# Attention's output kept as features by queries, with the RMS factors as rows through DRAM

## The chip, the cores and the metric

The kernel runs on one core of one Trainium2 chip. The core has five engines with a queue each: PE (TensorE, matmuls; its weight loads are listed as PEld and overlap), DVE (VectorE), ACT (ScalarE), POOL (GpSimd) and SP (SyncE, which here only issues DMAs). Each takes its instructions in program order; they meet by semaphores. The metric is the device time of one execution in microseconds (us), the median of several.

## The reference

One layer of a diffusion backbone for 256 prompt tokens and 2048 sample tokens with 512 cached keys; 1024 features, 4 attention heads of width 128. The part that matters here is differential attention, its sub-norm and the output projection:

```python
s = einsum('bqhmd,bkhmd->bhmqk', q, k) * scale     # two score maps, m = 0, 1
p = softmax(s, axis=-1)
a = p[:, :, 0] - lam * p[:, :, 1]
o = einsum('bhqk,bkhe->bqhe', a, v)                # 128 features a head
a = rms_norm(o, subln_g) * (1.0 - lam_init)        # over the 128 features
x = x + g1 * (concatenate([a.reshape(b, n, 512), four], axis=-1) @ w_out)
```

The other 512 columns of the concatenation (`four`) come from a Fourier mixing done earlier. An MLP follows. Everything is float32 at the borders; most products are done as three matmuls of a high and a low part (`mm3`).

## The kernel before

The stages follow each other: modulation, norm and input projection, Fourier mixing, attention (about 553 to 1245 us of the profiled execution), W_out (to about 1470), MLP.

**Attention.** A head has 8 groups of 256 sample queries (`Group`), and one group of the 256 prompt queries (`Prompt`). A group has two halves j of 128 queries. For each j and each map m there are five blocks b of 512 keys: `fill` (PE writes scores to one of five PSUM banks, tag "S"), `rowmax` and `comb` (DVE), `exp` (ACT, which frees the bank). When both maps of a half are done, `combine` adds them: two sums on DVE, then six POOL operations, of which four are large. Then `tr` transposes the result, `ah` (ACT) and `al` (DVE) split it, and `mul` sums features x queries into columns 0:256 of the PSUM bank that `PRO()` returns, the one all groups share; the prompt has columns 256:512 of it. The end of a group is o1 to o6: o1, ACT copies to `oT`; o2, PE transposes it back, two of 128x128; o3, DVE copies to `o` (queries x features); o4, ACT squares with accumulation, two; o5, DVE and a pow on POOL (L91, `pow_mhalf`); o6, POOL scales the rows by their factors, two, and SP stores them to `att`, one DRAM tensor for each 128 tokens.

**What sets the order.** The attention stage is written as a list of (time, function). `add(t, fn)` appends, the list is sorted by time, and the functions run in that order; so each engine's program order is fixed, and an engine that waits holds all that stands behind it. One step T is 5.2, a group takes four; u = T/5. In such units after the start of its last part (w, L1335) a group has o1 at 0, o2 at 0.4, o3 at 4.25, o4 at 8.5, o5 at 9.2, o6 at 9.6; w of the next group is 20 later. The prompt's own end falls at group 5 of its head (G[5]). Tiles come from pools: a tag has `bufs` buffers, taken in turn, and a new tile of the tag waits until the readers of the one that had its buffer are done. The default of pool `at` is two. The last group of the last head (`gr.last`) leaves o2 to o6 to the list `LASTO`, which the W_out stage calls; there POOL also issues the DMAs.

**W_out.** For each of 18 tiles of 128 tokens, `mix_load` (L1558) loads `am` from `att` and four 128-feature blocks of `mT` from `four`; `mix` (L1565) transposes `am` on PE (four of 128x128), ACT copies with the sub-norm's gain (`cols[:, 96:97]`, features on partitions) into `mT`, DVE splits `mT`; `out_mm` multiplies with the split weights that `w_split` (L1540) makes once. The first tile's transposes stand at the end of attention (`mix0_load`, `mix0_tr`, `mix0_copy`).

Of the kernel before, what the change touches and what calls it, by code (L numbers as in the profile page):

```python
# [11 lines left out]
F32 = mybir.dt.float32  # L12
# [25 lines left out]
def f32(ap):  # L38
    return ap.bitcast(F32)


def body(tc, a, out):
    nc = tc.nc
    ctx = ExitStack()
    with ctx:
# [6 lines left out]
        def scratch(name, shape):  # L52
            return dram.tile(shape, F32, tag=name, name=name)
# [8 lines left out]
        att = [scratch(f"att{i}", [P, 512]) for i in range(NT // P)]  # L62
# [926 lines left out]
        with ExitStack() as c3_:  # L989
# [49 lines left out]
            class Group:  # L1039
# [133 lines left out]

                def o2(self):
                    for j in range(2):
                        nc.tensor.transpose(self.po[:, 256 + j * P:256 + j * P + P], self.oT[:, j * P:j * P + P], ident)

                def o3(self):
                    self.o = self.op.tile([P, 256], F32, tag="o", name=f"o{self.nm}")
                    nc.vector.tensor_copy(self.o, self.po[:, 256:512])  # L1180

                def o4(self):
                    osq = self.op.tile([P, P], F32, tag="osq", name=f"osq{self.nm}", bufs=1)
                    self.oss = self.op.tile([P, 4], F32, tag="oss", name=f"oss{self.nm}")
                    for j in range(2):
                        nc.scalar.activation(osq, self.o[:, j * P:j * P + P], AF.Square, accum_out=self.oss[:, j:j + 1])

                def o5(self):
                    nc.vector.scalar_tensor_tensor(self.oss[:, 0:2], self.oss[:, 0:2], 1.0 / P, self.s0e, op0=ALU.mult, op1=ALU.add)
                    pow_mhalf(self.oss[:, 2:4], self.oss[:, 0:2], 2)  # L1190

                def o6(self):
                    for j in range(2):
                        c = slice(j * P, j * P + P)
                        nc.gpsimd.tensor_scalar(self.o[:, c], self.o[:, c], self.oss[:, 2 + j:3 + j], 0.0, op0=ALU.mult, op1=ALU.add)
                        (nc.gpsimd if self.last else nc.sync).dma_start(att[self.hd.tok0 + self.g * 2 + j][:, self.hd.hc], self.o[:, c])

            class Prompt(Group):
# [39 lines left out]
                def mul(self, j):  # L1238

                    (ah, al), V = self.A[0], self.hd.V  # L1240
                    n = 0
                    for t in range(2):
                        c = slice((t * 2 + j) * P, (t * 2 + j) * P + P)
                        for l, r in ((ah[:, c], V[:, t, 0, :]), (ah[:, c], V[:, t, 1, :]), (al[:, c], V[:, t, 0, :])):
                            n += 1
                            nc.tensor.matmul(PRO()[:, 256 + j * P:256 + j * P + P], l, r, start=False, stop=(n == 6), skip_group_check=True)

                def o3(self):
                    self.o = self.op.tile([P, 256], F32, tag="o", name=f"o{self.nm}")
                    nc.vector.tensor_copy(self.o, PRO()[:, 256:512])  # L1250

# [9 lines left out]
            def load_wout():  # L1261
                ak = aks[0]
                wv = a["w_out"][0].rearrange("(k p) n -> p k n", p=P)
                ts = [ak.tile([P, NK[0]], F32R, tag=f"KS{m}_0", name=f"wout{m}") for m in range(2)]
                ts.append(ak.tile([P, NK[0] // P, 2, P], F32R, tag="V_0", name="wout2").rearrange("p t x e -> p (t x e)"))
                for n, k in ((0, 0), (0, 1), (1, 2), (1, 3), (2, 4), (2, 5), (2, 6), (2, 7)):
                    w = f32(ts[n])[:, k % 2 * D:k % 2 * D + D] if n < 2 else f32(ts[n])[:, (k - 4) * D:(k - 3) * D]
                    nc.sync.dma_start(w, wv[:, k, :])
                    WOUT.append(w)

                MIX0.extend((f32(ts[0])[:, 2 * D:2 * D + 512], f32(ts[2])[:, 4 * D:5 * D].rearrange("p (k t) -> p k t", t=P)))
                nc.sync.dma_start(MIX0[1][:, 4:8, :], four[:, 0:P].rearrange("(k p) t -> p k t", p=P))

            def mix0_load():
                nc.sync.dma_start(MIX0[0], att[0])

            def mix0_tr(gr):
                MIX0.append(gr.bank("pmx0", "pt"))
                for k in range(4):
                    nc.tensor.transpose(MIX0[2][:, k * P:k * P + P], MIX0[0][:, k * P:k * P + P], ident)  # L1280

            def mix0_copy():
                nc.scalar.activation(MIX0[1][:, 0:4, :].rearrange("p k t -> p (k t)"), MIX0[2], AF.Copy, scale=cols[:, 96:97])

            for h in range(H):
# [237 lines left out]
        with c3o, ExitStack() as c4, ExitStack() as c4x, ExitStack() as c4w:  # L1523
# [16 lines left out]
            def w_split(hf, k0=0, k1=KD):  # L1540
                c = slice(hf * 512, hf * 512 + 512)
                wh, wl = WO[hf]
                for k in range(k0, k1):
                    nc.scalar.copy(wh[k], WOUT[k][:, c])
                    nc.vector.tensor_sub(wl[k], WOUT[k][:, c], f32(wh[k]))
# [12 lines left out]
            def mix_load(i):  # L1558
                am = tx.tile([P, 512], F32, tag="am", name=f"am{i}")
                nc.sync.dma_start(am, att[i])  # L1560
                mT = tx.tile([P, 8, P], F32, tag="mT", name=f"mT{i}")
                nc.sync.dma_start(mT[:, 4:8, :], four[:, i * P:i * P + P].rearrange("(k p) t -> p k t", p=P))
                M[i] = am, mT

            def mix(i):  # L1565
                if i == s0:
                    mT = MIX0[1]
                else:
                    am, mT = M[i]
                    pm = PRO().rearrange("p (k t) -> p k t", t=P)  # L1570
                    for k in range(4):
                        nc.tensor.transpose(pm[:, k, :], am[:, k * P:k * P + P], ident)
                    nc.scalar.activation(mT[:, 0:4, :], pm, AF.Copy, scale=cols[:, 96:97])
# [558 lines left out]
```

## Time and profile before

| what | us |
|---|---|
| median of 3 runs | 2862.14 (2862.11 to 2862.57) |
| span of the profiled execution | 2861.4 |
| PE busy | 2831.7 (99%) |
| DVE, ACT, POOL busy | 2018.0, 1548.2, 1073.3 |
| attention, 553 to 1245 | 692, of which PE is busy 689.0, POOL 627.5 |
| W_out, 1250 to 1480 | 230, of which PE is busy 227.2 |

In the profile's lines, L1172 is line 1172 of the kernel before; in a line of operations stand the start, the duration, the engine, the line, output <- inputs by their names (numbers left out: `oTs` is the sample's `oT` of any head and group, `oTp` the prompt's), the shape, and in brackets an idle time before it with what ended it. A line of waits has who waits, for whom, the us in total, how often, and the longest. PE's rows overlap, since matmuls are pipelined: what a matmul costs is the step from one start to the next.

### The profile page before, as it was taken

How to read it: one execution, taken by the hardware profiler on the slowest of the kernel's cores; microseconds unless marked ns; L12 is line 12 of the kernel's file. 1: busy time of each engine (PE TensorE's matmuls, PEld its weight loads, DVE VectorE, ACT ScalarE, POOL GpSimd, SP SyncE). 2: the span in 40 equal slices, each digit the busy share in tenths (PEclk: the TensorE clock that was granted, in tenths of full speed). 3: DMA queues.
4: the chain of work that ended last, by engine and by line, in shares of the span. 5: the costliest groups of instructions: out<-in, count | busy, mean ns of one | idle time of the engine just before them, and what ended most of it. 6: DMA issues, size and time to landing. Idle time of an engine off the chain costs nothing.

```text
span 2861.4 us, 43224 instructions
## 1 busy us (share of the span) xinstructions
PE 2831.7 (99%) x15109; PEld 2455.9 (86%) x15109; DVE 2018.0 (71%) x3393; ACT 1548.2 (54%) x3505; POOL 1073.3 (38%) x890
## 2 busy tenths in 40 slices
PE   8999999999999999999999999999999999999999
PEld 5888888688888888888889999999998888888887
DVE  7767886898988989864477777778775354345554
ACT  4333323798989989853356565556555332333221
POOL 1211223798999989942223333333332000000000
PEclk9999999999999999999999999999999999999999
DMA  7776777421211212036767676667747464445663
GB/s 284 219 207 198 230 213 237 172 106 38 73 71 53 106 38 99 23 124 201 242 221 232 223 246 228 221 219 238 234 167 255 147 202 135 138 144 185 206 206 111
DMA packets 392780, 492.94 MB, mean 172 GB/s; under 512 B 26467, under 2 KB 306384, under 8 KB 389490
## 3 DMA queue, kind: packets, MB, share of 16 engines
q1 hardware_dynamic: 387136, 479.73, 50.9%
q0 software_dynamic: 1872, 7.28, 0.8%
q10 hardware_dynamic: 3554, 3.17, 0.4%
q8 instruction: 119, 1.95, 0.3%
q14 instruction: 99, 0.81, 0.1%
HBM read 312.58 MB, written 179.59 MB: 172 GB/s over the span
## 4 chain that ended last, share of the span: by engine, by line
PE 54%; DVE 1%; DMA 0%; ACT 0%; issue 0%; SPq 0%; POOL 0%; DVEq 0%; POOLq 0%
PE ps L94 8%; PE ps L95 8%; PE ps L96 8%; PE pB L1749 2%; PE pB L1747 2%; PE pB L1748 2%; PE pA L1748 2%; PE pC L1748 2%; PE pA L1749 2%; PE pC L1747 2%; PE pA L1747 2%; PE pC L1749 2%; PE po L94 2%; PE po L96 2%; PE po L95 2%; PE pD L1749 1%
## 5 line engine op out<-in xcount | busy, mean ns | idle before, releaser
L1085 DVE TENSOR_REDUCE mxs<-Ss 128x1 f32<-128x512 f32 x636 | 405.4, 686 | 65.5 <-PE Ss L1080 55.1
L1420 DVE TENSOR_TENSOR sl<-sr,sh 128x768 fp32r<-128x768 f32 x168 | 161.8, 964 | 331.5 <-ACT sh L1419 331.1
L1120 POOL TENSOR_TENSOR P0s<-P0s,P1s 128x1024 f32<-128x1024 f32 (+2 forms) x128 | 378.6, 2958 | 10.7
L1419 ACT CAST sh<-sr 128x768 fp32r<-128x768 f32 x168 | 140.6, 838 | 418.3 <-PE ps L95 418.3
L1789 POOL TENSOR_TENSOR gs<-g,g 128x384 f32<-128x384 f32 x48 | 69.7, 1452 | 468.5 <-ACT g L1759 418.9
L1104 ACT ACTIVATE P1s<-Ss,mxs 128x512 f32<-128x512 f32 x318 | 215.4, 694 | 36.3 <-DVE mxs L1088 35.3
L94 PE MATMUL pj<-wh,hh 128*128 128x512 f32 x576 | 228.8, 397 | 2.0 <-DVE hh L555 2.0
L94 PE MATMUL ps<-thT,sh 128*128 128x512 f32 x585 | 227.6, 389 | 0.0
L95 PE MATMUL ps<-tlT,sh 128*128 128x512 f32 x585 | 227.6, 389 | 0.0
L96 PE MATMUL ps<-thT,sl 128*128 128x512 f32 x585 | 227.6, 389 | 0.0
L95 PE MATMUL pj<-wl,hh 128*128 128x512 f32 x576 | 227.1, 394 | 0.5 <-DVE wl L516 0.5
L96 PE MATMUL pj<-wh,hl 128*128 128x512 f32 x576 | 225.6, 392 | 0.0
L1104 ACT ACTIVATE P0s<-Ss,mxs 128x512 f32<-128x512 f32 x318 | 214.3, 691 | 5.6 <-DVE mxs L1088 5.0
L1135 PE MATMUL pts<-ident,P0s 128*128 128x128 f32 x1280 | 191.7, 273 | 4.5 <-DVE als L1147 1.8
L1080 PE MATMUL Ss<-KS0s,Qs 128*128 128x512 f32 x636 | 190.1, 419 | 0.4 <-ACT P1s L1104 0.4
L1080 PE MATMUL Ss<-KS1s,Qs 128*128 128x512 f32 x636 | 188.7, 420 | 1.5 <-ACT P0s L1104 1.4
L1758 ACT ACTIVATE g<-uz 128x384 f32<-128x384 f32 x144 | 75.7, 526 | 200.2 <-DVE uz L1781 174.1
L1135 PEld LDWEIGHTS pts<-ident,P0s 128*128 128x128 f32 x1280 | 151.3, 140 | 35.9 <-issue 4.8
L1119 POOL TENSOR_SCALAR P1s<-P1s,tots 128x1024 f32<-128x1024 f32 (+2 forms) x128 | 171.9, 1343 | 5.8
L1147 DVE TENSOR_TENSOR als<-pts,ahs 128x512 fp32r<-128x512 f32 x256 | 165.9, 681 | 6.9 <-ACT ahs L1142 6.7
L94 PE MATMUL ps<-ophT,sh 128*128 128x512 f32 x423 | 164.7, 389 | 1.1 <-DVE uz L1781 1.1
L96 PE MATMUL ps<-ophT,sl 128*128 128x512 f32 x423 | 164.6, 389 | 0.0
(536 smaller groups left out, 8073.9 us busy)
## 6 DMA issues: line engine op xcount, KB each, us to landing
sr<-sd SPq DMA_DIRECT2D x84, 768.0 KB, 4.5
a<-in_w SPq DMA_DIRECT2D x184, 256.0 KB, 4.2
sd<-gs SPq DMA_DIRECT2D x192, 192.0 KB, 1.9
sd<-g SPq DMA_DIRECT2D x144, 192.0 KB, 2.1
wm<-in_w_mod SPq DMA_DIRECT2D x32, 512.0 KB, 5.2
Qs<-qd SPq DMA_DIRECT2D x32, 512.0 KB, 4.0
b<-in_w SPq DMA_DIRECT2D x64, 256.0 KB, 5.8
b<-tsum SPq DMA_DIRECT2D x64, 256.0 KB, 4.7
```

The source lines that it names most:

```text
L94: nc.tensor.matmul(ps, lh, rh, start=first, stop=False)
L95: nc.tensor.matmul(ps, lh, rl, start=False, stop=False)
L96: nc.tensor.matmul(ps, ll, rh, start=False, stop=last)
L1080: nc.tensor.matmul(S[:, :w], self.Q[:, x, m, j * P:j * P + P], self.hd.KS[m][:, b * 512:b * 512 + w], start=(x == 0), stop=(x == 1))
L1085: nc.vector.tensor_reduce(self.mx[j][:, m, b:b + 1], self.S[j, m, b], axis=AX.X, op=ALU.max)
L1104: nc.scalar.activation(dst, S, AF.Exp, bias=self.mx[j][:, m, 6:7], accum_out=self.sm[j][:, m, b:b + 1])
L1119: nc.gpsimd.tensor_scalar(p, p, tot[:, 3:4], 0.0, op0=ALU.mult, op1=ALU.add)
L1120: nc.gpsimd.tensor_add(d, d, p)
L1135: nc.tensor.transpose(pt[:, c:c + P], self.p0[j][:, (kb + t) * P:(kb + t + 1) * P], ident)
L1747: nc.tensor.matmul(ps, wh[:, c], hh[:, k, :], start=first and k == 0, stop=False, skip_group_check=True)
L1748: nc.tensor.matmul(ps, wh[:, c], hl[:, k, :], start=False, stop=False, skip_group_check=True)
L1749: nc.tensor.matmul(ps, wl[:, c], hh[:, k, :], start=False, stop=k == 3, skip_group_check=True)
```

## The change

A group's output stays as `oT`, features x queries. The squares are taken by ACT straight from PSUM (`oq`, into `osq`), two matmuls against ones sum them over the features (o2: 128 queries x 1), DVE adds epsilon (o5), POOL does the pow (`opow`). The 256 factors go to a DRAM row (o6), come back as that row on all partitions (o7, tile `rb`), POOL multiplies `oT` by it (o8), and one store puts the features' rows into `att`, now one 512 x 256 tensor for each 256 tokens. `osq` and `rb` are tiles of one tag, "rb", with two buffers; `oT` has two buffers as before. The prompt gets the same steps, and its products the same orientation (six matmuls of 256 columns for twelve of 128). At W_out, `mT` is loaded directly; the sub-norm's gain goes into the weights of the first four blocks in `w_split`. The line numbers grow by one or so.

```diff
-        att = [scratch(f"att{i}", [P, 512]) for i in range(NT // P)]
+        att = [scratch(f"att{i}", [512, 2 * P]) for i in range(NT // 256)]
+        rsd = [scratch(f"rs{h}", [NT // 256, 256]) for h in range(H)]
...
+                def oq(self):
+                    self.osq = self.op.tile([P, 256], F32, tag="rb", name=f"osq{self.nm}", bufs=2)
+                    nc.scalar.activation(self.osq, PRO()[:, 256 * self.hd.s:256 * self.hd.s + 256], AF.Square)
+
                 def o2(self):
                     for j in range(2):
-                        nc.tensor.transpose(self.po[:, 256 + j * P:256 + j * P + P], self.oT[:, j * P:j * P + P], ident)
...
+                        nc.tensor.matmul(PRO()[:, 256 + 2 * self.hd.s + j:257 + 2 * self.hd.s + j], self.osq[:, j * P:j * P + P], ones, start=True, stop=True)
+
+                def o5(self):
                     self.oss = self.op.tile([P, 4], F32, tag="oss", name=f"oss{self.nm}")
...
+                    nc.vector.scalar_tensor_tensor(self.oss[:, 0:2], PRO()[:, 256 + 2 * self.hd.s:258 + 2 * self.hd.s], 1.0 / P, self.s0e, op0=ALU.mult, op1=ALU.add)
+
+                def opow(self):
                     pow_mhalf(self.oss[:, 2:4], self.oss[:, 0:2], 2)
 
+                def place(self):
+                    return nc.gpsimd if self.last else nc.sync, self.hd.tok0 // 2 + self.g
+
                 def o6(self):
...
+                    q, n = self.place()
+                    q.dma_start(rsd[self.hd.h][n].rearrange("(j p) -> p j", p=P), self.oss[:, 2:4])
+
+                def o7(self):
+                    q, n = self.place()
+                    self.rb = self.op.tile([P, 256], F32, tag="rb", name=f"rb{self.nm}", bufs=2)
+                    q.dma_start(self.rb, rsd[self.hd.h][n:n + 1].partition_broadcast(P).rearrange("p o d -> p (o d)"))
+
+                def o8(self):
+                    q, n = self.place()
+                    nc.gpsimd.tensor_mul(self.oT, self.oT, self.rb)
+                    q.dma_start(att[n][self.hd.hc], self.oT)
...
-                for t, fn, *args in ((0.25, gp.tr, 0), (0.9, gp.ah), (1.4, gp.al), (15.4, gp.mul, 0), (17.0, gp.mul, 1),
-                                     (20.85, gp.o3), (39.5, gp.o4), (40.2, gp.o5), (40.6, gp.o6)):
-                    add(G[5] + (t - 5 if h == H - 1 and t > 30 else t) * u, fn, *args)
+                for t, fn, *args in ((0.25, gp.tr, 0), (0.9, gp.ah), (1.4, gp.al), (17.0, gp.mul), (20.85, gp.oq), (21.3, gp.o1),
+                                     (28.61, gp.o2), (30.3, gp.o5), (35.25, gp.opow), (37.0, gp.o6), (41.0, gp.o7),
+                                     (45.25 if h == H - 1 else 55.25, gp.o8)):
+                    add(G[5] + t * u, fn, *args)
...
-                    for t, fn in ((0, gr.o1), (0.4, gr.o2), (0.75 if gr.last else 4.25, gr.o3), (8.5, gr.o4), (9.2, gr.o5), (9.6, gr.o6)):
-                        if gr.last and t:
+                    for t, fn in ((0, gr.oq), (0.4, gr.o1), (2.6, gr.o2), (4.25, gr.o5), (9.2, gr.opow), (11.0, gr.o6), (14.0, gr.o7), (19.2, gr.o8)):
+                        if gr.last and t > 1:
                             LASTO.append(fn)
...
-            add(base + T + 0.7 * u, mix0_load)
-            add(base + (AVS - 1) * T + 2.5 * u, mix0_tr, gr)
-            add(base + (AVS - 1) * T + 4.45 * u, mix0_copy)
...
+            add(base + (AVS - 2) * T + 0.7 * u, mix0_load)
...
+                    if k < H:
+                        nc.scalar.activation(wh[k], WOUT[k][:, c], AF.Copy, scale=cols[:, 96:97])
+                        nc.vector.scalar_tensor_tensor(wl[k], WOUT[k][:, c], cols[:, 96:97], f32(wh[k]), op0=ALU.mult, op1=ALU.subtract)
...
-                    am, mT = M[i]
-                    pm = PRO().rearrange("p (k t) -> p k t", t=P)
-                    for k in range(4):
-                        nc.tensor.transpose(pm[:, k, :], am[:, k * P:k * P + P], ident)
-                    nc.scalar.activation(mT[:, 0:4, :], pm, AF.Copy, scale=cols[:, 96:97])
```

How the instructions stand on their engines, at three places around the end of a group. In the names, `s0_5` is the sample's group 5 of head 0, the numbers behind are the buffers' own; the brackets list what an instruction waits for: an engine, or a hardware DMA queue (DMAHW). First ACT at the end of group 5 of head 0, before:

```order
L1104 ACTIVATE P1s0_7_1_0_7343,sms0_7_1_7210<-Ss0_7_1_1_0_7284,mxs0_7_1_7209 128x512 [waits DVE_49,Pool_49]
L1104 ACTIVATE P1s0_7_1_0_7343,sms0_7_1_7210<-Ss0_7_1_1_1_7299,mxs0_7_1_7209 128x512
L1172 COPY oTs0_5_7359<-po_5307 128x256 [waits PE_49]
L1104 ACTIVATE P1s0_7_1_1_7362,sms0_7_1_7210<-Ss0_7_1_1_2_7304,mxs0_7_1_7209 128x512 [waits Pool_49]
L1104 ACTIVATE P1s0_7_1_1_7362,sms0_7_1_7210<-Ss0_7_1_1_3_7314,mxs0_7_1_7209 128x512
L1104 ACTIVATE P1s0_7_1_1_7362,sms0_7_1_7210<-Ss0_7_1_1_4_7320,mxs0_7_1_7209 128x512
L1142 COPY ahs0_6_4_7385<-pts0_6_4_7348 128x512 [waits PE_49]
```

and with the change:

```order
L1105 ACTIVATE P1s0_7_1_0_7322,sms0_7_1_7184<-Ss0_7_1_1_0_7261,mxs0_7_1_7183 128x512 [waits DVE_49,Pool_49]
L1105 ACTIVATE P1s0_7_1_0_7322,sms0_7_1_7184<-Ss0_7_1_1_1_7278,mxs0_7_1_7183 128x512
L1177 ACTIVATE osqs0_5_7340<-po_5302 128x256 [waits DMAHW6_49,PE_49,Pool_49]
L1105 ACTIVATE P1s0_7_1_1_7343,sms0_7_1_7184<-Ss0_7_1_1_2_7283,mxs0_7_1_7183 128x512
L1173 COPY oTs0_5_7345<-po_5302 128x256 [waits DMAHW7_49]
L1105 ACTIVATE P1s0_7_1_1_7343,sms0_7_1_7184<-Ss0_7_1_1_3_7293,mxs0_7_1_7183 128x512
L1105 ACTIVATE P1s0_7_1_1_7343,sms0_7_1_7184<-Ss0_7_1_1_4_7299,mxs0_7_1_7183 128x512
L1143 COPY ahs0_6_4_7366<-pts0_6_4_7329 128x512 [waits PE_49]
```

The copy that waited for PE only is now two instructions around an exponential: the square, which waits for PE, POOL and a DMA, and the copy, which waits for another DMA. Between the two and behind them stand three exponentials, then the copies `ahs`. Next POOL between the pow of group 4 and the second combine of group 7, before:

```order
L91 TENSOR_TENSOR osss0_4_7181<-osss0_4_7181,mhalf_180 128x2 [waits DVE_49]
L1195 TENSOR_SCALAR os0_4_7115<-os0_4_7115,osss0_4_7181 128x128 [waits DMAHW4_49,DMAHW3_49,Pool_49]
L1195 TENSOR_SCALAR os0_4_7115<-os0_4_7115,osss0_4_7181 128x128
L1111 TENSOR_SCALAR tots0_7_0_7051<-tots0_7_0_7051,nlam_188 128x1 [waits DVE_49]
L1112 TENSOR_SCALAR s0es0_7_6820<-tots0_7_0_7051 128x1
L1119 TENSOR_SCALAR P1s0_7_0_0_7187<-P1s0_7_0_0_7187,tots0_7_0_7051 128x1024 [waits Activation_49,Pool_49]
L1120 TENSOR_TENSOR P0s0_7_0_7111<-P0s0_7_0_7111,P1s0_7_0_0_7187 128x1024 [waits PE_49,Pool_49]
L1119 TENSOR_SCALAR P1s0_7_0_1_7216<-P1s0_7_0_1_7216,tots0_7_0_7051 128x1536 [waits Activation_49]
L1120 TENSOR_TENSOR P0s0_7_0_7111<-P0s0_7_0_7111,P1s0_7_0_1_7216 128x1536 [waits Pool_49]
L1111 TENSOR_SCALAR tots0_7_1_7211<-tots0_7_1_7211,nlam_188 128x1 [waits DVE_49]
```

and with the change:

```order
L92 TENSOR_TENSOR osss0_4_7104<-osss0_4_7104,mhalf_175 128x2 [waits DMAHW5_49]
L1112 TENSOR_SCALAR tots0_7_0_7038<-tots0_7_0_7038,nlam_183 128x1 [waits DVE_49]
L1113 TENSOR_SCALAR s0es0_7_6811<-tots0_7_0_7038 128x1
L1120 TENSOR_SCALAR P1s0_7_0_0_7172<-P1s0_7_0_0_7172,tots0_7_0_7038 128x1024 [waits Activation_49,Pool_49]
L1121 TENSOR_TENSOR P0s0_7_0_7100<-P0s0_7_0_7100,P1s0_7_0_0_7172 128x1024 [waits PE_49,Pool_49]
L1120 TENSOR_SCALAR P1s0_7_0_1_7190<-P1s0_7_0_1_7190,tots0_7_0_7038 128x1536 [waits Activation_49]
L1121 TENSOR_TENSOR P0s0_7_0_7100<-P0s0_7_0_7100,P1s0_7_0_1_7190 128x1536 [waits Pool_49]
L1204 TENSOR_TENSOR oTs0_4_7047<-oTs0_4_7047,rbs0_4_7249 128x256 [waits DMAHW7_49,DMAHW6_49]
L1112 TENSOR_SCALAR tots0_7_1_7185<-tots0_7_1_7185,nlam_183 128x1 [waits DVE_49]
```

The two scalings stood right behind the pow; the one product stands behind a whole combine. Last PE, behind the transposes `pts0_5_4`, at the o2 of group 4, before:

```order
L1080 MATMUL Ss0_7_0_0_0_7052<-KS0s0_5262,Qs0_7_6818 128x512 x2
L1176 MATMUL po_5307<-ident_175,oTs0_4_7055 128x128 x2
L1080 MATMUL Ss0_7_0_0_1_7062<-KS0s0_5262,Qs0_7_6818 128x512 x2
L1080 MATMUL Ss0_7_0_0_2_7067<-KS0s0_5262,Qs0_7_6818 128x512 x2
L1135 MATMUL pts0_5_6_7070<-ident_175,P0s0_5_0_6512 128x128
L1135 MATMUL pts0_5_6_7070<-ident_175,P0s0_5_1_6663 128x128
L1135 MATMUL pts0_5_6_7070<-ident_175,P0s0_5_0_6512 128x128
L1135 MATMUL pts0_5_6_7070<-ident_175,P0s0_5_1_6663 128x128
L1080 MATMUL Ss0_7_0_0_3_7077<-KS0s0_5262,Qs0_7_6818 128x512 x2
L1080 MATMUL Ss0_7_0_0_4_7083<-KS0s0_5262,Qs0_7_6818 128x512 x2
```

and with the change:

```order
L1081 MATMUL Ss0_7_0_0_0_7039<-KS0s0_5257,Qs0_7_6809 128x512 x2
L1081 MATMUL Ss0_7_0_0_1_7049<-KS0s0_5257,Qs0_7_6809 128x512 x2
L1081 MATMUL Ss0_7_0_0_2_7054<-KS0s0_5257,Qs0_7_6809 128x512 x2
L1136 MATMUL pts0_5_6_7057<-ident_170,P0s0_5_0_6505 128x128
L1136 MATMUL pts0_5_6_7057<-ident_170,P0s0_5_1_6648 128x128
L1136 MATMUL pts0_5_6_7057<-ident_170,P0s0_5_0_6505 128x128
L1136 MATMUL pts0_5_6_7057<-ident_170,P0s0_5_1_6648 128x128
L1081 MATMUL Ss0_7_0_0_3_7064<-KS0s0_5257,Qs0_7_6809 128x512 x2
L1081 MATMUL Ss0_7_0_0_4_7070<-KS0s0_5257,Qs0_7_6809 128x512 x2
L1181 MATMUL po_5302<-ones_177,osqs0_4_7042 128x1 x2
```

The two transposes stood between the first and the second block of scores; the two matmuls against ones stand behind the fifth.

More of the change, by code (lines that the diff above doesn't have):

```diff
@@ L1236, in al, with mul, o1 @@
                     self.A[0].append(t)
-                def mul(self, j):
+                def mul(self):
                     (ah, al), V = self.A[0], self.hd.V
-                    n = 0
                     for t in range(2):
[L1243 to L1250, printed above, removed]
+                        c = slice(t * 256, t * 256 + 256)
+                        for n, (l, r) in enumerate(((0, ah), (1, ah), (0, al))):
+                            nc.tensor.matmul(PRO()[:, 256:512], V[:, t, l, :], r[:, c], start=False, stop=(t == 1 and n == 2), skip_group_check=True)
+                def o1(self):
+                    self.oT = self.op.tile([P, 256], F32, tag="oT", name=f"oT{self.nm}", bufs=2)
+                    nc.scalar.copy(self.oT, PRO()[:, 256:512])
             ev = []
@@ L1269, in load_wout @@
                     WOUT.append(w)
[L1271 to L1272 removed]
+                MIX0.append(f32(ts[2])[:, 4 * D:5 * D].rearrange("p (k t) -> p k t", t=P))
+                nc.sync.dma_start(MIX0[0][:, 4:8, :], four[:, 0:P].rearrange("(k p) t -> p k t", p=P))
             def mix0_load():
[L1275 to L1283 removed]
+                nc.sync.dma_start(MIX0[0][:, 0:4, :], att[0][:, 0:P].rearrange("(k p) t -> p k t", p=P))
             for h in range(H):
```

30 lines of the change are left out of this document (7 added, 23 removed).

## The prediction

> **What bounds the kernel now.** I read the page from the top: the busy shares, then the chain that ended last, then the busy time by stage, then the waits and the order of events inside one group.
>
> ```profile
> span 2861.4 us, 43224 instructions
> PE 2831.7 (99%) x15109; PEld 2455.9 (86%) x15109; DVE 2018.0 (71%) x3393; ACT 1548.2 (54%) x3505; POOL 1073.3 (38%) x890
> PE 54%; DVE 1%; DMA 0%; ACT 0%; issue 0%; SPq 0%; POOL 0%; DVEq 0%; POOLq 0%
> ```
>
> TensorE works for 99% of the span and holds the chain of waits. So an edit pays only if it takes work or a pause from PE, and costs only if it makes PE pause. The median of the runs, 2862.14, is 0.7 us above the span; I add 0.7 at the end.
>
> The change touches two stages, attention and W_out. Their busy times (window, then PE, PEld, DVE, ACT, POOL, and the granted clock):
>
> ```profile
> 553.00:1245.00 692.00, 689.01 (x4473) 583.69 (x4471) 610.04 (x1196) 619.56 (x1729) 627.51 (x506) 1.00 0.19 65
> 1250.00:1480.00 230.00, 227.21 (x1112) 190.64 (x1110) 128.65 (x170) 96.61 (x212) 59.63 (x54) 1.00 0.69 220
> ```
>
> The share of POOL, 38% overall, misleads: in attention it is 627.5 of 692 us, and ACT and DVE stand near it. Four engines run there with a tenth of slack, so one engine's lateness can reach the others. In W_out only PE is full.
>
> **What goes.** In W_out, four transposes for each of 17 tiles, and four more ahead of the stage:
>
> ```profile
> 1249.11 0.60 PE L1572 MATMUL po<-ident,am 128*128 128x128 f32 x4
> L1572 PE MATMUL po<-ident,am x68: 270/272/273, 1249.1 to 1449.2; 128*128 128x128 f32 x68
> ```
>
> Four take 0.60 us, of which 0.27 is the pipelined end of the last, so one costs PE 0.11; 72 give **-7.9**. The scaling that ACT did behind them moves into the split of the weights, which is done once, with DVE at 129 and ACT at 97 of 230 us to hide it. Without that cover, eight dearer DVE operations of a few tenths each would cost 2 us at most; I count nothing.
>
> In a group's o2, PE waits for ACT's copy, transposes twice and goes on:
>
> ```profile
> PEld po L1176 <- ACT oTs L1172: 13.0, 32, 0.7
> 684.06 0.71 PE L1080 MATMUL Ss<-KS0s,Qs 128*128 128x512 f32 x2
> 684.74 0.44 PE L1176 MATMUL po<-ident,oTs 128*128 128x128 f32 x2
> 684.94 1.22 PE L1080 MATMUL Ss<-KS0s,Qs 128*128 128x512 f32 x4
> 29.61 1.03 PE L537 MATMUL pm<-sums,quad 128*128 128x12 f32 x8 [0.17 <-DVE sums L528]
> ```
>
> The wait for the copy is 13.0 us over 32 groups, 0.4 each, half of it under the matmul before. The N=1 matmuls against ones come after two more blocks of scores, when the squares are long there. Their size is not in the trace; eight with 12 columns took 1.03 us, so two cost 0.11 each, as the two transposes do. What goes is the exposed wait, between 0 and 0.3 a group; the ACT copy, now one activation later, holds part of it back. I take 0.15 for 30 groups: **-4.5** (bounds 0 and -9).
>
> The prompt's twelve products of 128 columns become six of 256.
>
> ```profile
> 688.83 0.28 PE L94 MATMUL po<-ahs,Vs 128*128 128x256 f32 x1
> 688.95 0.28 PE L95 MATMUL po<-als,Vs 128*128 128x256 f32 x1
> 678.64 0.42 DVE L1250 COPY op<-po 128x256 f32<-128x256 f32 x1
> L1186 ACT ACTIVATE osqs<-os 128x128 f32<-128x128 f32 x62 | 20.5, 331 | 1.0
> ```
>
> Products of 256 columns follow each other by 0.115, of 128 columns by 0.11 (as the transposes above): 12 x 0.11 - 6 x 0.115 = 0.63 goes, and the prompt's two ones matmuls add 0.22. Over four heads: **-1.7**. DVE loses a copy of 0.42 and ACT, per group, two squares of 0.33 against one twice as wide; neither is the bound by itself, so I count nothing. POOL trades two scalings for one product:
>
> ```profile
> 1179.85 0.73 POOL L1226 TENSOR_TENSOR P0p<-P0p,P1p 128x256 f32<-128x256 f32 x1
> DMA to landing us min/median/max: 1.5/1.6/5.8
> ```
>
> The two scalings took 0.72 (a row below), the product 0.73: an equal trade in length. The second row is the stores to att: 1.6 us from issue to landing, 5.8 at worst.
>
> **The new wait.** Squares (osq) and factors (rb) share two buffers of one tag. In most groups they alternate and nothing waits. The prompt, once a head, puts its own squares in between at group 5 and shifts the rotation: ACT's square of group 5 then gets the buffer from which POOL's product of group 4 reads, and that of group 6 the one of group 5's product. These are the waits on POOL and on a DMA in the order rows of the section above: twice a head, 8 times in all. The product stands on POOL behind the pow and a whole combine. At group 5 of head 0 the trace of before gives all times:
>
> ```profile
> 684.32 0.37 ACT L1172 COPY oTs<-po 128x256 f32<-128x256 f32 x1
> 684.58 0.70 ACT L1104 ACTIVATE P1s<-Ss,mxs 128x512 f32<-128x512 f32 x1
> 685.25 0.70 ACT L1104 ACTIVATE P1s<-Ss,mxs 128x512 f32<-128x512 f32 x1
> ...
> 676.82 0.70 POOL L91 TENSOR_TENSOR osss<-osss,mhalf 128x2 f32<-128x2 f32 x1
> 679.44 0.34 POOL L1111 TENSOR_SCALAR tots<-tots,nlam 128x1 f32<-128x1 f32 x1 [1.11 <-DVE tots L1110]
> ...
> 685.44 3.51 POOL L1120 TENSOR_TENSOR P0s<-P0s,P1s 128x1536 f32<-128x1536 f32 x1
> ```
>
> ACT reaches the square where the copy stood, 684.32. The combine cannot start earlier: it waited 1.11 us for DVE's sums, so what POOL no longer does ahead of it is no gain. It ends at 688.95, the product 0.73 later, 689.7: ACT waits **5.0 to 5.4**. Queued behind on ACT are three exponentials and the casts for the next products; PE's next scores want the PSUM banks which those three would free:
>
> ```profile
> PEld Ss L1080 <- ACT P0s L1104: 17.2, 53, 0.4
> ```
>
> Today that wait (53 times, 17.2 us in all) is 0.4 us at the longest, so PE follows ACT closely, with no stock to live on. Moreover the copy oT takes its buffer from the product two groups ago (the prompt's shifts this rotation too, to the last group), whose store must land first: 1.6 us after the product, with one exponential in between, so another 0.3 to 0.8. PE loses 5.4 to 6.3; I take 6.0. Group 6 looks alike: the combine ahead of its product ends 5.7 after its copy, less the 1.4 of four scalings (two here, two of the group) that stand ahead of it before and go.
>
> ```profile
> 706.77 0.37 ACT L1172 COPY oTs<-po 128x256 f32<-128x256 f32 x1
> ...
> 702.26 0.72 POOL L1195 TENSOR_SCALAR op<-op,ossp 128x128 f32<-128x128 f32 x2
> ...
> 708.97 3.54 POOL L1120 TENSOR_TENSOR P0s<-P0s,P1s 128x1536 f32<-128x1536 f32 x1
> ```
>
> Can the time be won back? PE is busy 99.6% of the stage; no. Three heads, two waits: 6 x 6.0 = **+36.0** (bounds 30 and 39).
>
> In head 3 the prompt's product comes early and the scores run out:
>
> ```profile
> 1219.99 0.37 ACT L1172 COPY oTs<-po 128x256 f32<-128x256 f32 x1
> 1224.58 0.33 POOL L1111 TENSOR_SCALAR tots<-tots,nlam 128x1 f32<-128x1 f32 x1
> 1232.95 0.37 ACT L1172 COPY oTs<-po 128x256 f32<-128x256 f32 x1 [1.39 <-PE po L96]
> 1232.99 0.69 POOL L91 TENSOR_TENSOR osss<-osss,mhalf 128x2 f32<-128x2 f32 x1
> DMA to landing us min/median/max: 3.1/3.4/3.7
> ```
>
> The first wait is as before, 1224.58 + 0.73 against 1219.99, 5.1 on PE. At the second the pow of group 5 starts only when ACT is ready, and the whole way by DRAM is bare: pow 0.7, store of the factors 1.6, load 3.4 (an estimate from the loads of mT, the last row), product 0.73, so 1239.4 against 1232.95: 6.5. Together **+11.6** (10 to 14). Elsewhere store and load, 5.0, lie under the 9.5 us of the combine between pow and product, and nobody waits. On SP a group's two stores become store, load, store, and SP waits in line for pow, landing and product. Behind stand mainly the Q loads:
>
> ```profile
> Qs<-qd SPq DMA_DIRECT2D x32, 512.0 KB, 4.0
> ```
>
> They are issued three steps of 5.2 us ahead of the first scores, 15.6; 4.0 of landing and some 5 of SP's wait fit in. I count nothing; a Q load that came late would hold PE for the difference.
>
> **The clock.** What does a pause of 5 us do to PE's clock? The nearest rows are at the start of the kernel:
>
> ```profile
> 32.62 0.79 PE L94 MATMUL pj<-wh,hh 128*128 128x512 f32 x1 [1.98 <-DVE hh L555]
> 33.21 0.63 PE L95 MATMUL pj<-wl,hh 128*128 128x512 f32 x1
> 33.64 0.63 PE L96 MATMUL pj<-wh,hl 128*128 128x512 f32 x1
> 1250.01 0.40 PE L96 MATMUL po<-woh,ml 128*128 128x512 f32 x1
> 1250.24 0.39 PE L94 MATMUL po<-woh,mh 128*128 128x512 f32 x1
> 30.88:37.71 6.83, 5.09 (x12) 3.98 (x13) 6.62 (x15) 6.71 (x16) 0.93 (x1) 0.50 0.84 318
> ```
>
> After light work and an idle 1.98 us the granted clock was 0.50 for 6.8 us; matmuls started 0.43 us apart instead of 0.23 as in W_out, and twelve cost 2.3 us too much. Behind the new pauses ACT paces the scores at 0.67 us a block, which hides a part. Between 0 and 2.3 for each of 8, I take 1.2: **+9.6**. The Trainium skill ("TensorE: Matmul & The Clock Gate", Part 1, What's actually happening) has the clock at half after an idle window of about 3.4 us, until some 3.4 us of sustained work; its section Why this matters for your kernels warns of idle gaps over some 3 us between bursts. By that rule every pause here, over 5 us, halves the clock, and the sum would hold 18.4 in place of 9.6, 2914; the trace agrees as far as it goes, with half the clock after less than that, and only a clock that stays at 1.00 would give 2895.
>
> **Sum.** 36.0 + 11.6 + 9.6 - 7.9 - 4.5 - 1.7 = +43.1 on 2861.4, and 0.7: **2905**.
>
> **Rivals.** *The waits do not bite.* If the product were ready when ACT comes, only savings would be left: 2862.1 - 14.1 = 2848, faster. That turns on one number, the combine's end after ACT's copy; it must shrink from 4.6 to under zero, or PE have 5 us of scores in stock. The share of 99% and the longest wait of 0.4 speak against it. Chance 0.08. *Shorter waits:* ACT and DVE lose work, so PE may work ahead of the square and the pause shrink to 3.5 us, too short for the clock: 6 x 3.5 + 8 - 14.1 = +15, 2877; chance 0.10. For the total to stay within 0.2% (5.7 us, about what a measurement here can tell) the pause would have to be some 2 us: 0.03. *The factors come late:* if store and load each took the 5.8 us that the slowest store did, 11.6 would exceed the combine's 9.5 and POOL would wait 2 us in each of 32 groups; POOL, 90% busy, has 2 us to give, so at most half shows: about 2935. The median of 1.6 speaks against: 0.04. The forecast keeps 0.75.
>
> **Range.** Low: waits 5.0 to 5.5 and no clock loss give 2890, and the case of shorter waits 2877. High: clock 18.4, waits 6.5, head 3 at 14 give 2920. I give 2876 to 2922. Faster 0.08, within 0.2% 0.03, slower 0.89.
>
> **What would show it.** In ACT's waits of the new trace: the squares' line behind POOL's product, 8 times, 5 us each, at groups 5 and 6 of each head and nowhere else; PE idle there, and granted clock under 1 in those windows alone. W_out's transposes gone and that stage 7 us shorter. If the squares wait for nothing, or PE works on behind them, the forecast is wrong from the ground; if pauses are there with clock 1.00, it is 10 us too high.

## The result, and the profile after

The changed kernel takes 3000.4 us (median of 5; 2999.4 to 3007.0) against 2862.6: ratio 1.0486, 95% interval 1.0473 to 1.0499, so some 138 us slower. The profiled execution has a span of 2997.7. The first page lines after the change:

```profile
span 2997.7 us, 43127 instructions
PE 2855.9 (95%) x15093; PEld 2475.9 (83%) x15093; DVE 1990.3 (66%) x3357; ACT 1524.1 (51%) x3383; POOL 1065.2 (36%) x855
PEclk9999999998998998998999999999999999999999
```

Every engine but PE has less work, and PE, 99% before, has pauses. The time by stage, the same two windows before and after (from the first scores to W_out's first matmul, and from there to its last), is in the first column after the window:

```profile
517.10:1381.50 864.40, 747.48 (x4630) 625.61 (x4630) 622.41 (x1224) 634.95 (x1711) 648.07 (x487) 0.94 0.20 65
1381.50:1602.40 220.90, 215.45 (x1006) 177.66 (x1005) 112.51 (x162) 79.15 (x188) 54.96 (x55) 0.98 0.74 222
...
518.50:1245.20 726.70, 718.39 (x4580) 599.69 (x4580) 641.16 (x1259) 648.61 (x1813) 650.51 (x523) 1.00 0.20 72
1245.20:1467.30 222.10, 220.27 (x1071) 183.11 (x1070) 121.13 (x163) 91.05 (x211) 59.63 (x54) 1.00 0.68 217
```

The first two rows are of after, the last two of before. All of the loss lies in attention, 864.4 against 726.7. PE is idle there for 117 us (864.4 - 747.5) against 8; the other 29 is longer busy time, most of it matmuls at half clock (mean 0.94): the trace's record of the clock has eleven stretches at 0.50 there, in which PE worked for 44 us and so lost 22. W_out, in which a twelfth stretch falls, is only 1.2 us shorter.

The waits of after in that stretch (who, for whom, us in total, times, longest):

```profile
POOL oTs L1204 <- DMA rbs<-rs: 125.4, 31, 13.1
ACT osqs L1177 <- POOL oTs L1204: 82.9, 8, 11.6
PE Ss L1081 <- ACT P1s L1105: 66.7, 26, 11.8
PE po L1181 <- ACT oTs L1173: 24.4, 3, 12.5
ACT oTs L1173 <- DMA att<-oTs: 6.1, 8, 1.4
PE Ss L1081 <- DMA Qs<-qd: 4.3, 1, 4.3
```

The eight waits of ACT's square for POOL's product are there, and PE's behind them; but each takes 10.4 us, not 5.3, and above them stands a row that the forecast had at nothing: the product waits for the load of the factors in 31 groups. The last row is a Q load that came late once, a case that the forecast named and priced at nothing; it is absent where the factors come in time (the fifth and the eleventh run below). At group 5 of head 0, ACT, PE, POOL and SP (rows of their timelines, one after the other):

```profile
687.55 0.68 ACT L1105 ACTIVATE P1s<-Ss,mxs 128x512 f32<-128x512 f32 x1
699.82 0.38 ACT L1177 ACTIVATE osqs<-po 128x256 f32<-128x256 f32 x1 [11.50 <-POOL oTs L1204]
...
687.95 1.19 PE L1081 MATMUL Ss<-KS0s,Qs 128*128 128x512 f32 x4
700.93 1.22 PE L1081 MATMUL Ss<-KS0s,Qs 128*128 128x512 f32 x2 [11.79 <-ACT P1s L1105]
...
686.21 0.69 POOL L92 TENSOR_TENSOR osss<-osss,mhalf 128x2 f32<-128x2 f32 x1
692.84 3.42 POOL L1121 TENSOR_TENSOR P0s<-P0s,P1s 128x1536 f32<-128x1536 f32 x1
699.07 0.72 POOL L1204 TENSOR_TENSOR oTs<-oTs,rbs 128x256 f32<-128x256 f32 x1 [2.81 <-DMA rbs<-rs]
...
686.93 0.37 SPq L1195 DMA_DIRECT2D rs<-osss  x1
694.43 0.32 SPq L1200 DMA_DIRECT2D rbs<-rs  x1
```

ACT came to the square at 688.33. The combine ahead of the product ended 7.9 later (692.84 + 3.42; POOL had fallen behind through the same waits in the groups before), the product then waited 2.81 for the row, and took 0.72: 11.5. The row was late because the load could only be issued 7.5 us after the store (7.5 to 9.9 over all groups), since SP waits for that to land. The store's own view says it plainly; for after, and for the fifth run below, in which the pieces are 128 of 8 bytes:

```profile
DMA to landing us min/median/max: 7.9/8.6/9.7
...
DMA to landing us min/median/max: 2.7/3.2/8.8
```

### The profile page after: what moved, and what is told of

The parts are those of the page before. It is cut to its first block, busy times and chain, and to the rows that moved or that the text cites. A ratio compares the mean times of both kernels' runs of the same rounds, so it can differ in the third digit from the quotient of the medians.

```text
span 2997.7 us, 43127 instructions
## 1 busy us (share of the span) xinstructions
PE 2855.9 (95%) x15093; PEld 2475.9 (83%) x15093; DVE 1990.3 (66%) x3357; ACT 1524.1 (51%) x3383; POOL 1065.2 (36%) x855
## 4 chain that ended last, share of the span: by engine, by line
PE 51%; DVE 1%; DMA 0%; issue 0%; ACT 0%; SPq 0%; POOL 0%; DVEq 0%; POOLq 0%
PE ps L95 8%; PE ps L96 8%; PE ps L97 8%; PE pB L1741 2%; PE pB L1739 2%; PE pB L1740 2%; PE pC L1739 2%; PE pA L1739 2%; PE pA L1740 2%; PE pC L1741 2%; PE pA L1741 2%; PE pC L1740 2%; PE po L97 2%; PE po L96 2%; PE po L95 2%; PE pD L1741 1%
## 5 line engine op out<-in xcount | busy, mean ns | idle before, releaser
L1081 PE MATMUL Ss<-KS0s,Qs 128*128 128x512 f32 x636 | 202.9, 438 | 71.8 <-ACT P1s L1105 67.0
L1136 PE MATMUL pts<-ident,P0s 128*128 128x128 f32 x1280 | 199.5, 280 | 17.8 <-POOL P0s L1121 13.1
L1081 PEld LDWEIGHTS Ss<-KS0s,Qs 128*128 128x128 f32 x636 | 106.7, 197 | 114.2 <-ACT P1s L1105 94.9
L1136 PEld LDWEIGHTS pts<-ident,P0s 128*128 128x128 f32 x1280 | 158.6, 146 | 43.7 <-POOL P0s L1121 14.8
L1143 ACT CAST ahs<-pts 128x512 fp32r<-128x512 f32 x256 | 148.6, 612 | 70.1 <-PE pts L1136 70.0
```

The lines of the kernel that those rows point to most:

```text
L1081: nc.tensor.matmul(S[:, :w], self.Q[:, x, m, j * P:j * P + P], self.hd.KS[m][:, b * 512:b * 512 + w], start=(x == 0), stop=(x == 1))
L1136: nc.tensor.transpose(pt[:, c:c + P], self.p0[j][:, (kb + t) * P:(kb + t + 1) * P], ident)
```

## The experiments

Theory S: ACT's waits through the shared turn of the buffers, made longer by late factors. Theory R: POOL itself, waiting for the factors with no slack, costs as much without ACT's waits. The eleventh run, which prices the forecast's own terms, stands last. All medians stand beside 2863 of the kernel before on the same chip.

**Buffers of the prompt's own** (squares and factors in the tag of the second map's scores, the copy in that of the first).

```diff
-  tag="rb", ... bufs=2                  # osq and rb
+  tag=("rb", "P1_1")[self.hd.s], ... bufs=2 - self.hd.s
-  tag="oT"                              # the prompt's oT
+  tag="P0_1"
```

> The prompt's squares, factors and output copy take buffers that the prompt has already (those of its two score maps), so the sample's groups keep their turn in the two-buffer tags. Theory S (the shared turn): the added time sits in the 8 waits of ACT for POOL's product; without the shifted turn they go, groups 5 and 6 of each head fall from 32 to 36 us to what the other late groups take (23 to 26), 97 us in all, and the time is 2895 to 2910. Theory R (POOL's pace): what costs is POOL, which waits about 4 us for the factors in each group and has no slack; the shared buffers only show it. Then groups 5 and 6 stay several us too long without any wait of ACT, and the time is 2930 to 2970.

2937.2: 63 less than the change, in R's range. ACT's eight waits are gone, but the product's remain, and PE waits more for what POOL does late (the second row; 14.8 us in 8 waits in the change):

```profile
POOL oTs L1204 <- DMA rbs<-rs: 117.9, 29, 15.0
PEld pts L1136 <- POOL P0s L1121: 32.5, 15, 4.6
```

So the late factors cost on their own too.

**A row that was there long before.** The kernel leaves out the normalisation: the product reads a row that holds no factors.

```diff
-  q.dma_start(self.rb, rsd[self.hd.h][n:n + 1].partition_broadcast(P)...)
+  q.dma_start(self.rb, four[n:n + 1, 0:256].partition_broadcast(P)...)
```

> The product's row is loaded from a fixed row of DRAM that has long been there, so the load waits for no store of factors; the store itself stays. The output is not normalised. The shifted turn stays. Theory S: the waits of ACT remain 8, but each is the 5 to 5.5 us that the combine ahead of the product makes, 40 to 45 us in all against 83, POOL's wait for the factors goes, and the time is 2885 to 2910, near the forecast. Theory R: once POOL no longer waits, the kernel is near the one before, 2850 to 2872. Third, if the load and not the store is what is late, POOL still waits and the time stays over 2970.

2949.0, 40 over the range of S: the eight waits fell to 48.9 us in all, about as expected, but in seven groups POOL still waits for the row (26.5 us in all). SP's rows at group 5 of head 0 show why, and POOL's product with them:

```profile
708.91 0.37 SPq L1195 DMA_DIRECT2D rs<-osss  x1
709.58 0.37 SPq L1195 DMA_DIRECT2D rs<-ossp  x1
710.12 0.34 SPq L1200 DMA_DIRECT2D rbs<-four  x1
...
719.72 0.73 POOL L1204 TENSOR_TENSOR oTs<-oTs,rbs 128x256 f32<-128x256 f32 x1 [0.74 <-DMA rbs<-four]
```

The load, issued behind two stores of factors, needs 9.6 us though it waits for none of them by a semaphore: such stores seem to hold up what is issued behind them. Where the landing is in the trace, these loads took 7.1 to 12.2 us, against 4.0 to 8.2 in the change, where the load is issued after the store has landed. So this run took the dependence away, not the store's cost; the fifth and the eleventh run price that.

**Half of the first edit:** `osq` and `rb` on buffers of the prompt's own, `oT` not.

> Only the prompt's squares and factors get buffers of their own; its copy oT still shifts the turn of the sample's oT. Theory S says that the turn is shifted in two tags and either alone makes ACT wait: the wait moves from the square to the copy, one exponential later, and lasts until the product's store has landed: time 2985 to 3010. If only the tag of squares and factors matters, the time is that of the first run, some 2900.

3011.2: nothing gained. The wait moved to the copy, as S says, and ends when the product's store has landed:

```profile
ACT oTs L1173 <- DMA att<-oTs: 87.5, 8, 13.3
```

**Product later** (with the first edit).

```diff
-  (19.2, gr.o8)
+  (19.2 if h == H - 1 and g > 4 else 27.2, gr.o8)
```

> As the first run, and the product stands 8 units later, behind the second combine and just ahead of the next pow, some 19 us after its own pow; the last three groups of the last head keep the old place. Theory S: neither ACT nor POOL waits any more before the last head's end, only the savings are left: 2845 to 2862. Theory R: POOL no longer waits for the factors either, so the same; told apart from S by the first two runs. If something else is dear (the 4-byte stores slowing other transfers, SP's queue), the time stays above 2870.

2901.2: 36 less than the first run, so POOL's waiting was worth at least that, but 40 above the forecast of both theories; the third case, something else that is dear, had come in. Two things were left: every group took half a us longer than before, and ACT's copy waited for stores that landed late (12.0 us in 5 waits).

**The store in 128 pieces of 8 bytes** (with the first edit; product in its old place).

```diff
-  rsd[self.hd.h][n].rearrange("(j p) -> p j", p=P)
+  rsd[self.hd.h][n].rearrange("(p j) -> p j", j=2)
-  nc.gpsimd.tensor_mul(self.oT, self.oT, self.rb)
+  o = self.oT.rearrange("q (j p) -> q j p", p=P)
+  nc.gpsimd.tensor_mul(o, o, self.rb.rearrange("q (p j) -> q j p", j=2))
```

> As the first run (the prompt on buffers of its own, product at its old place), and the factors are stored as 128 pieces of 8 bytes in place of 256 of 4; the product reads the row in the other order. In the trace of the change the load of the row is issued 7.5 us after the store. Theory N (the number of pieces sets the store): 4 to 5 us now; with the load's 4 to 6 the row is there near the end of the combine, POOL's 121 us of waits in attention fall under 50, and the time goes from 2937 to 2895 to 2912. Theory F (a fixed time of such a store): 7 us or more remain, and the time stays within 5 us of 2937.

2876.5 (ratio 1.0051, 1.0036 to 1.0066): 61 less than the first run, more than the 25 to 42 expected. The store lands in 3.2 us (median), and POOL's wait for the factors is down from 118 us to two waits at the end of the stage:

```profile
POOL oTs L1205 <- DMA rbs<-rs: 18.1, 2, 11.5
```

**Square and copy behind the fifth exponential** (on the fourth run, then on the fifth).

```diff
-  (0, gr.oq), (0.4, gr.o1), ...      if gr.last and t > 1:
+  (1.66, gr.oq), (1.68, gr.o1), ...  if gr.last and t > 2:
```

> As the fourth run (late product, 2901), and ACT does the square and the copy together behind the fifth exponential of the wave, not between the second and fourth. In all runs so far a group without any long wait takes 22.55 us against 22.0 before. Theory X: these 0.55 are ACT's second operation among the exponentials, since PE's next scores follow them closely; behind the fifth it delays no bank, the group takes 22.0 to 22.15, and the time falls by 12 to 18 us, to 2883 to 2890. If the 0.55 come from elsewhere (the ones matmuls, DVE's reading of PSUM, the 4-byte stores), the groups stay at 22.5 and the time within 4 us of 2901.

> Both edits on the first run, product at its old place. If theories N and X hold and their gains add: 2937 - 32 - 16 = about 2889, 2878 to 2897. If only one holds, the time is that of the other run alone, 2900 to 2925.

2885.5, 15.7 less than the fourth, as theory X has it (the fourth's own runs spread over 10 us); and 2867.5 on the fifth (ratio 1.0013, 1.0004 to 1.0023), 9 less than the fifth and below the forecast's 2878, because the store's part was 61 and not 32. The place of ACT's copies in the first groups shows the pace (first and last start; of before, after, and the seventh run):

```profile
L1172 ACT COPY oTs<-po x4: 371/372/374, 572.1 to 638.2; 128x256 f32<-128x256 f32 x4
...
L1173 ACT COPY oTs<-po x3: 386/387/388, 571.7 to 616.9; 128x256 f32<-128x256 f32 x3
...
L1173 ACT COPY oTs<-po x3: 398/401/401, 573.2 to 617.5; 128x256 f32<-128x256 f32 x3
```

Three groups in 66.1 us are 22.03 each; two in 45.2 are 22.6; two in 44.3 are 22.15: of the 0.55 added, 0.45 is gone. PE's wait for ACT's exponentials of the second map, in the fourth and the sixth run, which differ in this place alone (in the sixth the ones matmuls wait for ACT instead, 13.0 us in 30 waits):

```profile
PEld Ss L1081 <- ACT P1s L1105: 43.8, 81, 3.4
...
PEld Ss L1081 <- ACT P1s L1105: 13.4, 52, 0.4
```

**The end mended** (on the seventh run): POOL issues the store of the last head's group 6, and that head's group 5 has its square and copy early again.

```diff
-  q.dma_start(att[n][self.hd.hc], self.oT)
+  (nc.gpsimd if self.drain else q).dma_start(att[n][self.hd.hc], self.oT)
...
-  (1.66, gr.oq), (1.68, gr.o1)
+  (0 if h == H - 1 and g == 5 else 1.66, gr.oq), (0.4 if h == H - 1 and g == 5 else 1.68, gr.o1)
```

> As the seventh run (2867.5), with two edits at the end of attention: POOL issues the store of the last head's group 6, so that SP does not stand behind it with the loads of W_out's second tile; and the squares and the copy of the last head's group 5 stand at their early place. In the seventh run PE stood 3.2 us for that second tile and 2.2 us for those squares, and the clock was at half for 3.4 us behind each. If these are the cause of what is left, 5 to 8 us go: 2859 to 2863, just under the kernel before; if the second tile is late for another reason (its own store), 2 to 3 go: about 2865.

2864.8 (1.0004, 0.9995 to 1.0013): no different from before. Of the 5 to 8 us hoped for, 2.8 went, the lesser case. W_out now takes 216.6 us against 222.1, with 6.8 us at half clock in it. Ahead of it PE stands 2.7 us for the first tile, whose prompt rows come by the same way over DRAM; DVE's split of it starts when they land:

```profile
1248.88 0.69 DVE L1569 CAST mh<-wout 128x1024 fp32r<-128x1024 f32 x1 [3.36 <-DMA wout<-att]
```

**Two stores of 128 pieces of 4 bytes** (on the seventh run; the product reads the row in the change's order again).

```diff
-  q.dma_start(rsd[...].rearrange("(p j) -> p j", j=2), self.oss[:, 2:4])
+  for j in range(2):
+      q.dma_start(rsd[...].rearrange("(j p) -> p j", p=P)[:, j:j + 1], self.oss[:, 2 + j:3 + j])
```

> As the seventh run, but the factors go to DRAM as 4-byte pieces again, in two stores of 128 pieces each (row order as in the change). Told apart: is the 256-piece store slow by the number of pieces of one store or by the size of a piece? If by the number in one store, each takes about 3.2 us as the 128 pieces of 8 bytes did, the second ends some 4 us after the first is issued, and the time is 2866 to 2876. If by the size of 4 bytes, each takes 7 us or more, POOL waits for the factors as in the change, and the time is 2895 or more.

2933.0. Each store of half the pieces still takes nearly all of the time, so it isn't the number of pieces in one store that is dear:

```profile
DMA to landing us min/median/max: 6.8/7.6/11.4
```

Whether it is the size of a piece, or that both stores together still bring 256 pieces at once, this run does not tell.

**Sums in one pass** (on the eighth run: squares and ones fp32r, two columns of ones), and the same with the addresses of all later tiles kept.

```diff
-  ..., self.osq[:, j * P:j * P + P], ones, ...
+  ..., self.osq[:, j * P:j * P + P].bitcast(F32R), onesr, ...
```

> As the eighth run, and the squares and the ones are fp32r (the squares are rounded when they are written; two equal columns of ones, of whose sums one is read). In the traces each float32 matmul against ones is two instructions with a weight load each, so a group's two cost PE 4 x 0.115 = 0.46, not the 0.22 of the prediction. As fp32r they are two instructions: 36 x 0.23 = 8 us less if PE's time is what counts: 2855 to 2860, below the kernel before. If the wait for the squares or ACT's pace counts instead, the time stays within 2 us of 2864.8.

> The tenth run with its new tile of ones taken out of a padding beside it, so that all later tiles in SBUF stand at the same addresses as in the eighth run. In the tenth run they stood 32 bytes higher, and matmuls in every stage took 1% longer (393 against 389 ns), outside attention too; that hid what the sums were to give. If the address was all, 2855 to 2860, under the kernel before; if one-pass sums give nothing, 2863 to 2867 as the eighth run; if the added time has another cause, 2880 or more.

2892.6 and 2861.9: the second's ratio to before is 0.9999 (0.9990 to 1.0008). The first was slower outside attention only: matmuls that it does not touch took longer (eighth, tenth and twelfth run, the same group of the MLP):

```profile
L95 PE MATMUL ps<-thT,sh 128*128 128x512 f32 x585 | 227.6, 389 | 0.0
...
L98 PE MATMUL ps<-thT,sh 128*128 128x512 f32 x585 | 230.0, 393 | 0.0
...
L98 PE MATMUL ps<-thT,sh 128*128 128x512 f32 x585 | 227.6, 389 | 0.0
```

The twelfth run's expectation says that this was so in every stage; it was not. In the tenth run the first scores came 8.7 us later than in the eighth (526.1 against 517.4), and from W_out's last matmul to the end it took 21.5 more (1416.5 against 1395.0); but the scores' matmuls took 397 ns and W_out's 389 (medians) in both, and attention 732.5 against 732.3. So the sums in one pass gained nothing in attention there, and with the addresses kept attention takes 731.2, about 1 us less, of the 8 expected. The twelfth run's median is 2.9 below the eighth's, but the intervals of their ratios to before overlap, so that gain is not shown. No version beat the kernel before by more than the measurement can tell.

**The shared turn with the factors in time** (the eleventh run: the change, with only the store of the fifth run).

> The change with only the store of the factors mended (128 pieces of 8 bytes); the prompt shifts the sample's turn as in the change. Against the fifth run, 2876.5, which differs in that turn alone, this prices the 8 waits where the factors are in time, which is what the prediction priced: 36.0 + 11.6 for the waits and 9.6 for the clock, 57. If those terms were right, 2925 to 2940, with ACT's 8 waits at 5 to 6 us each, 40 to 48 in all; the clock may add up to 15 more. If the waits are still near 10 us each, the late factors weren't what doubled them, and the time is over 2960.

2931.3, as forecast. ACT's eight waits are 4.7 us each, a little under the forecast's 5 to 6 (10.4 in the change, where the row comes late):

```profile
ACT osqs L1177 <- POOL oTs L1205: 37.7, 8, 5.9
```

## Why the prediction was wrong

Four runs make a square, in us:

| | store 256 x 4 bytes | store 128 x 8 bytes | the store's part |
|---|---|---|---|
| shared turn | 3000.4 (the change) | 2931.3 | 69 |
| prompt on its own buffers | 2937.2 | 2876.5 | 61 |
| the turn's part | 63 | 55 | |

The right column's 2876.5 is 13.8 above the kernel before (2862.7). So the 138 us are 69 for the late factors, 55 for the turn and 14 for savings that did not come, where the forecast had 0, 57 and -14.

**The waits and the clock: right in kind and in sum, and the sum in part by luck.** The forecast had 36.0 + 11.6 for the waits and 9.6 for the clock, 57 together; with the factors in time the turn costs 55, with eight waits in the places named, at groups 5 and 6 of each head. In head 3 the two pauses of PE are 5.9 and 5.8 us, the forecast's 11.6. The third run shows that the rotation of `oT` is as much a part of it as that of `osq` and `rb`. The square can't tell waits from clock, but the traces can. From the first scores to W_out's first matmul, with the turn (the eleventh run) and without it (the fifth):

```profile
517.90:1317.80 799.90, 746.59 (x4630) 627.99 (x4630) 622.41 (x1224) 633.04 (x1711) 648.03 (x487) 0.96 0.25 70
...
516.90:1261.50 744.60, 727.65 (x4631) 608.68 (x4630) 620.13 (x1224) 634.29 (x1718) 648.76 (x487) 1.00 0.27 75
```

PE is idle for 53.3 us against 17.0, 36 more where the waits were priced at 47.6; and it is busy for 18.9 more where the clock was priced at 9.6. The clock was at 0.50 in eight stretches, in which PE worked for 45.4 us and so lost up to 22.7. So the waits were some 11 too dear and the clock some 9 too cheap, and the two errors cancel; of the forecast's figures for the clock, the 18.4 of its upper case was the nearer. In the change itself the granted clock was 0.50 in twelve stretches. Eight begin inside the eight pauses, as at group 5 of head 0; the other four lie elsewhere, though the forecast expected them in those windows alone:

```profile
688.33:699.83 11.50, 0.80 (x4) 0.32 (x2) 1.29 (x2) 0.01 (x1) 8.48 (x5) 0.64 0.09 11
691.50:705.20 13.70, 4.27 (x15) 3.50 (x15) 1.83 (x3) 3.74 (x10) 5.39 (x3) 0.50 0.23 59
```

The clock fell 3.2 us after ACT had stopped and came back 5.4 after it went on; half of PE's 4.3 us of work in that time is the price, about 2. Over the eight it is 2.1 on average here and 2.8 in the eleventh run, so the forecast's bounds of 0 to 2.3 for one pause were too low. The stretches last 3.4, 6.8, 10.2 or 13.7 us: multiples of the window of some 3.4 us that the Trainium skill names ("TensorE: Matmul & The Clock Gate", Part 1, What's actually happening). On this point the trace agrees.

**The step that failed** is the sentence that the factors' store and load, 1.6 + 3.4, lie under the 9.5 us of the combine, and nobody waits. The store took 8.6 (median), five times the row that it was priced by, a store of 128 rows of 512 bytes; the load took 4.6 at the wait shown above, also more than its estimate. Together they pass 12 us. So the product was late in nearly every group: 61 to 69 us, as the square has it. This was the rival *the factors come late*, given 0.04 and 2935. Its mechanism was right, and so was its guess that half of POOL's waiting shows in the time; the size of the wait was not. It had 2 us in each of 32 groups; the change has 125.4 us in 31 groups, 4 each, and the first run 117.9 in 29. ACT's eight waits stand behind it and lengthen from 4.7 to 10.4, but that adds little: with the shared turn the late factors cost 69, without it 61. The store's upper bound, 5.8, came from the slowest of the 512-byte stores, and a store of single elements was in no row; the range should have been wider there for that reason.

**The savings: wrong in sign.** Forecast at -14.1; but the fifth run, free of both faults but for the end of head 3, is 13.8 slower than before: attention takes 744.6 us against 726.7, W_out 216.7 against 222.1. W_out's part is right in size where the clock holds: in the eleventh run, at 1.00 throughout the stage, it takes 214.2, 7.9 less than before, where 7.5 were forecast for the stage's own 68 transposes. In the groups, o2's 4.5 were a loss instead: even in the seventh run a group takes 0.12 us longer than before, some 4 us over 32.

```profile
L1181 PE MATMUL po<-ones,osqs 128*128 128x1 f32 x128 | 18.1, 245 | 24.4 <-ACT oTs L1173 24.4
```

The profile of after counts 128 matmuls against ones for 32 groups, four each where two were assumed (the twelfth run, with half of them, shows about 1 us of that). And ACT's square stands among the exponentials in addition to the copy. Moving both behind the fifth exponential gave 15.7 and 9 us; so the step "neither is the bound by itself, so I count nothing", said of DVE's and ACT's lighter work, failed in that place. PE follows ACT's exponentials within 0.4 us, as the forecast itself said, and there an ACT operation of 0.26 us (their starts' distance) can reach PE: the 0.45 us that a group regained is nearly that of the two operations moved.

**Head 3** lost more than the 11.6 in the change: two pauses of 12.5 and 11.6 us at the ones matmuls alone, where the run with the factors in time has 5.9 and 5.8. Its end is where the way over DRAM stays bare; PE's longest new pause in the eighth run, 2.7 us, is left there.

## What to carry to other kernels

A path over DRAM is priced by a row of the same shape, pieces and piece size, and where the trace has none its range must reach far beyond the nearest row; here 256 pieces of 4 bytes took 8.6 us, 128 of 8 bytes 3.2. When an extra user takes a turn in a tag of two buffers, look up whom the next user then waits for; waits in program order on an engine that others follow closely add to every lateness behind them. And an operation that is moved between others counts by what follows its engine at that place, not by the engine's share of busy time. Last, a sum that comes out right does not show that its terms are: each wants its own row, as the waits and the clock here.

## What the runs showed of the hardware

A store's bytes did not set its time: 1 KB took 8.6 us in 256 pieces of 4 bytes and 3.2 in 128 of 8, and a load issued behind two such stores was late with them. A shift of later SBUF tiles by 32 bytes made matmuls 1% longer in some stages (393 against 389 ns in the MLP) and not in others (397 ns for the scores in both runs), and the kernel some 30 us slower (2892.6 against 2861.9), with the same work; why is open. Behind eight PE pauses of 4.5 to 5.9 us the granted clock was at 0.50 for 3.4 to 10.2 us, and cost up to 2.8 us a pause on average (the eleventh run).
